# Layer 0 of a two-layer encoder: class heads' logits on the row halves of TensorE, values as the stationary operand on its column halves, head factors spread over channels through DRAM

## The chip, the core and the metric

The kernel runs on one core of one Trainium2 chip. A core has TensorE (PE; its weight loads are listed apart as PEld), VectorE (DVE), ScalarE (ACT), GpSimd (POOL) and SyncE (SP), whose queue issues nearly all of this kernel's transfers. TensorE multiplies a stationary operand that was loaded into its array (128 rows by 128 columns) by a moving operand and writes to PSUM; the other engines read PSUM and work in SBUF. The metric is the device time of one execution in microseconds, the median of several runs.

## The reference, cut to what matters

The input is 512 tokens of 1024 channels. Each of two layers is RMSNorm, a token mixer, a residual add, RMSNorm, a squared-ReLU MLP and a residual add; a final RMSNorm ends the network. The change lies in the mixer of layer 0, dilated sliding-window attention with 16 heads of 64 channels in three groups:

```python
A_GROUPS = ((128, 1, 6), (512, 4, 5), (2048, 16, 5))   # window, dilation, heads
# per group: keys at offsets -win/2 .. win/2 in steps of the dilation, a bias from rel_bias
lse = jax.nn.logsumexp(logits, axis=-1)
p = jnp.exp(logits - lse[..., None])
o = jnp.einsum('bhqk,bqkhd->bqhd', p, v_sel)
glses.append(jax.nn.logsumexp(lse, axis=-1) - math.log(nh))
...
alpha = jax.nn.softmax(jnp.stack(glses, axis=-1), axis=-1)
o = concatenate([outs[g] * (3 * alpha[..., g])[..., None, None] for g in range(3)])
return o.reshape(B, S, 16 * 64) @ w_o
```

So each head's output row (one token) is scaled by one factor, which needs the sums of all 16 heads at that token: the group's weight alpha times three, over the head's own softmax sum.

## The kernel before

**Linear products.** Activations are kept transposed, channels on partitions and the 512 tokens along the free axis, in eight tiles. A weight unit is 1 MB (1024 rows by 256 columns): SP loads it into `raw` (two buffers), ScalarE casts the high part `whi` (L156), VectorE subtracts the low part `wlo` (L157), and TensorE runs three products of 512 columns per step (`mm3`, L167 to L169) into a PSUM bank, `acc` (two banks) or `s_ps` (three).

**Heads in pairs.** The 16 heads are eight pairs p, two heads of 64 channels on one 128-partition tile. Pairs 0 to 2 are the window heads (dilation 1), pairs 3 to 7 the class heads: there tokens are sorted into four classes by their position modulo 4, so that a class of 128 queries meets a class of 128 keys. `qk0(j)` makes queries and keys of pairs 2j and 2j+1, `probs0(p)` the probabilities, `values0(j)` the values and the value products.

**Probabilities.** For a class head, `probs0` runs four products into one `s_ps` bank (L517, the head's 64 partitions as rows of the array, so half of it), one per class b; then per class VectorE adds the bias and takes a minimum, ScalarE takes the exponential and its sum (`softmax_block`); TensorE transposes the four blocks (L523) and VectorE copies them into `pt`, which has keys on partitions and queries along the free axis. Window heads do the same with two blocks of keys per class of queries.

**Values.** `out_v` scales the values, transposes them (L538, four 128x128 blocks), ScalarE copies them to `vn` (L540). The value product has `pt` as the stationary operand, 128x128, and 64 columns of `vn` as the moving one, so the result has queries on partitions (L548 for window heads, two products added up; L552 for class heads). ScalarE copies the bank `o_ps` (one buffer) to `o` (L555).

**Factors and output.** `group_stats` and `head_factors` make the factors with queries on partitions; the statistics of window and class heads sit in different token orders and are exchanged through small DRAM tiles (`exN`, `exS`, L606 to L618). The factors end in `sN` (window heads) and `sS` (class heads), a value per query, block and head. Then, per pair, VectorE multiplies `o` by the factors (L627), TensorE transposes the result back to channels on partitions (L630, four blocks), ScalarE casts the high part `oh` out of PSUM in the reference's token order (L638), VectorE subtracts the low part `ol` (L639), and the output projection `w_o` starts on them.

**Order.** A scheduler with a time model sets the order of instructions on every engine when the kernel is built; on the chip each engine runs its own in that order and waits on semaphores. Tiles come from pools with a fixed number of buffers, and the scheduler keeps the order in which they are asked for.

Of the kernel before, what the change touches and what calls it, by code (L numbers as in the profile page):

```python
# [82 lines left out]
def tile_encoder(ctx: ExitStack, tc: tile.TileContext, x, rel_bias, gains, norm_final_g,  # L83
# [383 lines left out]
    sN = l0p.tile([P, NB, 6], F32, name="sN", bufs=1)  # L467
    mnS = l0p.tile([P, NB, 10], F32, name="mnS", bufs=1)
    sS = l0p.tile([P, NB, 10], F32, name="sS", bufs=1)
# [15 lines left out]
    def probs0(p):  # L485
        for hh in range(2):
            h = 2 * p + hh
            rows = slice(64 * hh, 64 * hh + 64)
            q, k = qT[p], kT[p]
# [21 lines left out]
            else:  # L511
# [3 lines left out]
                S = s_tile().rearrange("p (u k) -> p u k", u=4)  # L515
                for b in range(NB):
                    nc.tensor.matmul(S[:, b, :], q[rows, b * P:(b + 1) * P], k[rows, (3 - b) * P:(4 - b) * P],  # L517
                                     start=True, stop=True)
                for b in range(NB):
                    softmax_block(S[:, b, :], Pt[:, b, :], B1[:, i, :], mnS[:, b, i:i + 1], sS[:, b, i:i + 1])  # L520
# [6 lines left out]
    def values0(j):  # L527
        def out_v(ct, ps):
# [12 lines left out]
            ops = o_tile().rearrange("p (b h e) -> p b h e", b=NB, h=2)  # L541
            for hh in range(2):
                h = 2 * p + hh
                pt = PT[h]
                for b in range(NB):
                    if p < 3:
                        for u in range(2):
                            nc.tensor.matmul(ops[:, b, hh, :], pt[:, 2 * b + u, :],  # L548
                                             v[:, (2 - b + u) % 4, 64 * hh:64 * hh + 64],
                                             start=u == 0, stop=u == 1)  # L550
                    else:
                        nc.tensor.matmul(ops[:, b, hh, :], pt[:, b, :], v[:, 3 - b, 64 * hh:64 * hh + 64],  # L552
                                         start=True, stop=True)
            o = hpool.tile([P, NB, 2, 64], F32, tag=f"Bl{p}", name=f"o{p}")
# [65 lines left out]
    head_factors(allN, [(sN, 0, 6, 0)])  # L620
    values0(2)
# [3 lines left out]
    for p in range(8):  # L625
        f = sN[:, :, 2 * p:2 * p + 2] if p < 3 else sS[:, :, 2 * p - 6:2 * p - 4]
        nc.vector.tensor_mul(O[p], O[p], bcast(f, 64))  # L627
        T = t_tile()
        for b in range(NB):
            nc.tensor.transpose(T[:, b * P:(b + 1) * P], O[p][:, b, :, :].rearrange("p h e -> p (h e)"), ident)  # L630
# [355 lines left out]
```

## Time and profile before

| | us |
|---|---|
| median of 3 runs | 1221.16 (1220.15 to 1221.30) |
| the profiled execution, its own time | 1220.61 |
| span in the trace | 1218.4 |
| TensorE busy | 1203.0 |
| VectorE busy | 628.9 |
| ScalarE busy | 500.6 |

The span runs from the first to the last instruction in the trace; the execution's time has 2.2 us more around it. Busy times count an instruction from start to end, and TensorE's overlap in its pipeline, so a busy time near the span tells that it rarely stands still and not how fast it could be. What a piece of work costs is read from the chain that ended last, in which each piece counts only what it adds.

### The profile page before, as it was taken

To read this page: it belongs to the slowest core of one execution; us is meant where nothing else is said; L and a number is where in the kernel's file an instruction comes from. 1 tells how busy PE (TensorE), PEld (TensorE's weight loads), DVE (VectorE), ACT (ScalarE), POOL (GpSimd) and SP (SyncE) were. 2 spreads that over 40 slices of the span, in tenths; PEclk is the share of its full clock that TensorE was granted. 3 is DMA by queue.
4 is the path that set the end of the run, shared out by engine and by line. 5 is a ranking of instruction groups with operands and counts; after the bars stand their busy time and mean duration, and the time that the engine had idled before them with its cause. 6 is when DMAs were issued, how large, how long until landed. Compare 5 with 4: busy or idle time off the path is not lost.

```text
span 1218.4 us, 15236 instructions
## 1 busy us (share of the span) xinstructions
PE 1203.0 (99%) x6124; PEld 1020.3 (84%) x6124; DVE 628.9 (52%) x1052; ACT 500.6 (41%) x922; POOL 87.5 (7%) x145
## 2 busy tenths in 40 slices
PE   9999999999999999999999999999999999999997
PEld 7788878888888888888888998987888888888897
DVE  5684455744433434434478677675744344334323
ACT  5462333443422413313357676654543224123133
POOL 0000000200000000000101212122200000000012
PEclk9999999999999999999999999999999999999999
DMA  7631222233322333223522333221333322333211
GB/s 226 117 104 36 70 70 70 73 100 104 104 89 84 104 104 104 94 80 104 150 75 94 100 115 107 74 85 54 102 104 104 104 88 86 104 105 104 88 51 70
DMA packets 107478, 115.72 MB, mean 95 GB/s; under 512 B 4703, under 2 KB 101087, under 8 KB 107359
## 3 DMA queue, kind: packets, MB, share of 16 engines
q1 hardware_dynamic: 107344, 114.48, 29.8%
q8 instruction: 48, 0.79, 0.3%
q0 software_dynamic: 64, 0.27, 0.1%
q14 instruction: 22, 0.18, 0.1%
HBM read 112.50 MB, written 2.24 MB: 94 GB/s over the span
## 4 chain that ended last, share of the span: by engine, by line
PE 95%; DMA 2%; DVE 1%; ACT 1%; issue 0%; POOL 0%; POOLq 0%; ACTq 0%; DVEq 0%
PE acc L167 15%; PE acc L169 15%; PE acc L168 15%; PE s_ps L167 13%; PE s_ps L168 13%; PE s_ps L169 13%; PE o_ps L833 2%; DMA raw<-in_a_w_qkv_dram 2%; PE s_ps L349 1%; PE s_ps L350 1%; PE t_ps L824 1%; PE o_ps L548 1%; PE s_ps L517 1%; PE o_ps L552 1%; PE t_ps L508 1%; PE t_ps L130 0%
## 5 line engine op out<-in xcount | busy, mean ns | idle before, releaser
L156 ACT CAST whi<-raw 128x1024 fp32r<-128x1024 f32 x188 | 188.3, 1049 | 399.1 <-PE s_ps L168 201.6
L157 DVE TENSOR_TENSOR wlo<-raw,whi 128x1024 fp32r<-128x1024 f32 x188 | 224.3, 1231 | 28.4 <-ACT whi L156 27.7
L167 PE MATMUL acc<-Ah,whi 128*128 128x512 f32 x472 | 185.5, 393 | 0.0
L168 PE MATMUL acc<-Al,whi 128*128 128x512 f32 x472 | 185.4, 393 | 0.0
L169 PE MATMUL acc<-Ah,wlo 128*128 128x512 f32 x472 | 185.1, 392 | 0.0
L167 PE MATMUL s_ps<-Ah,whi 128*128 128x512 f32 x352 | 137.4, 391 | 0.0
L168 PE MATMUL s_ps<-Al,whi 128*128 128x512 f32 x352 | 137.2, 390 | 0.0
L169 PE MATMUL s_ps<-Ah,wlo 128*128 128x512 f32 x352 | 136.9, 390 | 0.0
L169 PEld LDWEIGHTS acc<-Ah,wlo 128*128 128x128 f32 x472 | 88.7, 188 | 18.3
L167 PEld LDWEIGHTS acc<-Ah,whi 128*128 128x128 f32 x472 | 88.7, 188 | 18.1
L168 PEld LDWEIGHTS acc<-Al,whi 128*128 128x128 f32 x472 | 88.7, 188 | 17.6
L674 ACT ACTIVATE u<-u 128x512 f32<-128x512 f32 x64 | 40.0, 628 | 96.6 <-DVE u L673 95.9
L167 PEld LDWEIGHTS s_ps<-Ah,whi 128*128 128x128 f32 x352 | 66.1, 188 | 14.9 <-ACT Ah L230 0.5
L683 DVE TENSOR_TENSOR h<-h,s_ps 128x512 f32<-128x512 f32 x33 | 22.7, 687 | 108.0 <-PE s_ps L169 108.0
L168 PEld LDWEIGHTS s_ps<-Al,whi 128*128 128x128 f32 x352 | 66.1, 188 | 14.0 <-DVE lsum L392 0.5
L169 PEld LDWEIGHTS s_ps<-Ah,wlo 128*128 128x128 f32 x352 | 66.1, 188 | 13.7
L243 POOL TENSOR_TENSOR nacc<-nacc,nsq 128x512 f32<-128x512 f32 x18 | 27.4, 1525 | 548.5 <-ACT nsq L241 548.0
L673 DVE SCALAR_TENSOR_TENSOR u<-s_ps,rB 128x512 f32<-128x512 f32 x38 | 26.2, 691 | 76.0 <-PE s_ps L169 73.9
L168 PE MATMUL s_ps<-Bl,whi 128*128 128x512 f32 x152 | 59.1, 389 | 0.0
L167 PE MATMUL s_ps<-Bh,whi 128*128 128x512 f32 x152 | 59.1, 389 | 0.0
L169 PE MATMUL s_ps<-Bh,wlo 128*128 128x512 f32 x152 | 59.1, 389 | 0.0
L808 ACT ACTIVATE p<-p,st 128x512 f32<-128x512 f32 x64 | 46.2, 723 | 27.8 <-DVE st L805 27.0
(241 smaller groups left out, 2265.1 us busy)
## 6 DMA issues: line engine op xcount, KB each, us to landing
raw<-in_mlp_w_in_dram SPq DMA_DIRECT2D x32, 1024.0 KB, 5.3
raw<-in_mlp_w_out_dram SPq DMA_DIRECT2D x32, 1024.0 KB, 5.2
raw<-in_b_w_qkv_dram SPq DMA_DIRECT2D x12, 1024.0 KB, 5.1
raw<-in_a_w_qkv_dram SPq DMA_DIRECT2D x10, 1024.0 KB, 5.3
bias<-fd SPq DMA_DIRECT2D x16, 448.0 KB, 3.7
raw<-in_a_w_o_dram SPq DMA_DIRECT2D x4, 1024.0 KB, 5.1
raw<-in_b_w_o_dram SPq DMA_DIRECT2D x4, 1024.0 KB, 5.5
h<-in_x_dram SPq DMA_DIRECT2D x8, 256.0 KB, 4.1
```

Source lines behind the costliest of these rows:

```text
L156: nc.scalar.copy(hi[:, :, c], raw[:, :, c])
L157: nc.vector.tensor_sub(lo[:, :, c], raw[:, :, c], f32(hi[:, :, c]))
L167: nc.tensor.matmul(ps, ahi, bhi, start=first, stop=False)
L168: nc.tensor.matmul(ps, ahi, blo, start=False, stop=False)
L169: nc.tensor.matmul(ps, alo, bhi, start=False, stop=last)
L243: eng.tensor_add(self.acc, self.acc, sq)
L349: nc.tensor.matmul(S, q[m][:, qs], k[m][:, ks], start=True, stop=False)
L673: nc.vector.scalar_tensor_tensor(u, ps, 0.0, nm.rB, op0=ALU.max, op1=ALU.mult)
L674: nc.scalar.activation(u, u, AF.Square)
L683: nc.vector.tensor_add(hT[ct], hT[ct], ps)
L808: nc.scalar.activation(pt, xt, AF.Exp, bias=mn, scale=-1.0, accum_out=st[:, b, 2 + m:3 + m])
L833: marks["PV"] = nc.tensor.matmul(O[:, b, :], aT[:, k, :], v[:, k, es], start=k == 0, stop=k == NB - 1)
```

## The change

Four things change, all in layer 0.

1. For class heads, the logits of both heads of a pair are issued ahead of the two softmaxes, in turn: class b of the head on partitions 0 to 63, then of the head on 64 to 127. They go to two `s_ps` banks.
2. In the value product, the values are now the stationary operand (128 rows by 64 columns) and `pt` the moving one (128 columns). The result has channels on partitions. The two heads of a pair go to partitions 0 to 63 and 64 to 127 of one bank, so to the two column halves of the array, in turn.
3. The transposes of `o` (L630) go, since `o` has channels on partitions already.
4. The factors must therefore run along the free axis, the same for all 64 channels of a head. `sN` and `sS` become parts of one tile `sA`; TensorE transposes it once (64 rows: 16 heads by 4 blocks), ScalarE copies that to `fT`, SP writes it to a DRAM tile `fac`, and eight loads read it back, each row repeated on 64 partitions, into four tiles `fB` of two pairs each. `fB` uses the buffers of the window heads' `ptn`. The product with `o` is written over `fB`, and `oh` and `ol` are made from there, not from PSUM.

```diff
-    sN = l0p.tile([P, NB, 6], F32, name="sN", bufs=1)
+    sA = l0p.tile([P, 16, NB], F32, name="sA", bufs=1)
+    sN = sA[:, 0:6, :].rearrange("p h b -> p b h")
+    sS = sA[:, 6:16, :].rearrange("p h b -> p b h")
-    sS = l0p.tile([P, NB, 10], F32, name="sS", bufs=1)
...
+        if p >= 3:
+            S2 = [s_tile().rearrange("p (u k) -> p u k", u=4) for _ in range(2)]
+            for b in range(NB):
+                for hh, rows in enumerate((lo64, hi64)):
+                    nc.tensor.matmul(S2[hh][:, b, :], q[rows, b * P:(b + 1) * P], k[rows, (3 - b) * P:(4 - b) * P],
+                                     start=True, stop=True)
...
-                S = s_tile().rearrange("p (u k) -> p u k", u=4)
-                for b in range(NB):
-                    nc.tensor.matmul(S[:, b, :], q[rows, b * P:(b + 1) * P], k[rows, (3 - b) * P:(4 - b) * P],
-                                     start=True, stop=True)
...
-            ops = o_tile().rearrange("p (b h e) -> p b h e", b=NB, h=2)
-            for hh in range(2):
-                h = 2 * p + hh
-                pt = PT[h]
-                for b in range(NB):
-                    if p < 3:
-                        for u in range(2):
-                            nc.tensor.matmul(ops[:, b, hh, :], pt[:, 2 * b + u, :],
-                                             v[:, (2 - b + u) % 4, 64 * hh:64 * hh + 64],
-                                             start=u == 0, stop=u == 1)
-                    else:
-                        nc.tensor.matmul(ops[:, b, hh, :], pt[:, b, :], v[:, 3 - b, 64 * hh:64 * hh + 64],
-                                         start=True, stop=True)
+            ops = o_tile()
+            for b in range(NB):
+                for u in range(2 if p < 3 else 1):
+                    for hh, rows in enumerate((lo64, hi64)):
+                        if p < 3:
+                            a, w, last = PT[2 * p + hh][:, 2 * b + u, :], v[:, (2 - b + u) % 4, rows], u == 1
+                        else:
+                            a, w, last = PT[2 * p + hh][:, b, :], v[:, 3 - b, rows], True
+                        nc.tensor.matmul(ops[rows, b * P:(b + 1) * P], w, a, start=u == 0, stop=last)
...
+    fac = dram.tile([64, P], F32, name="fac")
+    T = t_tile()
+    nc.tensor.transpose(T[0:64, 0:P], sA.rearrange("p h b -> p (h b)"), ident)
+    fT = l0p.tile([64, P], F32, name="fT", bufs=1)
+    nc.scalar.copy(fT, T[0:64, 0:P])
+    nc.sync.dma_start(fac, fT)
+    F = []
+    for pp in range(4):
+        f = l0p.tile([P, 2, SEQ], F32, tag="ptn", name="fB", bufs=4)
+        for hh, rows in enumerate((lo64, hi64)):
+            a = fac[0:1, 0:1]
+            nc.sync.dma_start(f[rows], bass.AP(tensor=a.tensor, offset=a.offset + (4 * pp + hh) * SEQ,
+                                               ap=[[0, 64], [2 * SEQ, 2], [1, SEQ]]))
+        F += [f[:, 0, :], f[:, 1, :]]
     values0(2)
     values0(3)
...
-        f = sN[:, :, 2 * p:2 * p + 2] if p < 3 else sS[:, :, 2 * p - 6:2 * p - 4]
-        nc.vector.tensor_mul(O[p], O[p], bcast(f, 64))
-        T = t_tile()
-        for b in range(NB):
-            nc.tensor.transpose(T[:, b * P:(b + 1) * P], O[p][:, b, :, :].rearrange("p h e -> p (h e)"), ident)
+        nc.vector.tensor_mul(F[p], O[p], F[p])
...
-            vh, vl, tv = rev(hi[:, :]), rev(lo[:, :]), T
+            vh, vl, tv = rev(hi[:, :]), rev(lo[:, :]), F[p]
```

The scheduler sets the order anew. Up to the first class head's logits and from the last quarter of the output projection on, TensorE's order is the same; between them it moves at three places that matter here. Names ahead of the arrow are what is written; numbers in them tell buffers apart. A row stands for one product; in the trace an fp32 product of `s_ps` or `o_ps` is two passes.

The first place is TensorE at the logits of pair 5 (L517 before, L493 after), behind those of pair 4 and the value products of pair 2. Before:

```order
L517 MATMUL s_ps_1285<-k0_1124,q0_1062 128x128 x3
L548 MATMUL o_ps_1169<-vn_1167,ptn_872 128x64 x8
L548 MATMUL o_ps_1169<-vn_1167,ptn_907 128x64 x8
L538 MATMUL t_ps_1215<-ident_84,v0_1213 128x128 x4
L523 MATMUL t_ps_1252<-ident_84,psg_1233 128x128 x4
L517 MATMUL s_ps_1285<-k0_1124,q0_1062 128x128
L517 MATMUL s_ps_1310<-k0_1124,q0_1062 128x128 x4
L167 MATMUL acc_1341<-Ah0_126,whi_1127 128x512
```

After, from the transposes of pair 3's values on (s_ps_1282 is the bank of the pair's first head, s_ps_1283 that of the second):

```order
L541 MATMUL t_ps_1214<-ident_84,v0_1212 128x128 x4
L526 MATMUL t_ps_1256<-ident_84,psg_1242 128x128
L493 MATMUL s_ps_1283<-k0_1123,q0_1061 128x128 x2
L526 MATMUL t_ps_1256<-ident_84,psg_1242 128x128
L493 MATMUL s_ps_1283<-k0_1123,q0_1061 128x128
L493 MATMUL s_ps_1282<-k0_1123,q0_1061 128x128
L526 MATMUL t_ps_1256<-ident_84,psg_1242 128x128
L493 MATMUL s_ps_1283<-k0_1123,q0_1061 128x128
L526 MATMUL t_ps_1256<-ident_84,psg_1242 128x128
L167 MATMUL acc_1340<-Ah0_126,whi_1126 128x512
```

The five products that stood in one run now stand in three, with single transposes between. The heads of pairs 4 and 6 alternate as written; those of pairs 3 and 7 stand head by head, as before.

The second place is TensorE behind the linear products of pair 6's values (acc_1709 before, acc_1726 after), where the value products of pair 4 (heads 8 and 9, pt8 and pt9) stand. Before:

```order
L169 MATMUL acc_1709<-Ah7_133,wlo_1605 128x512
L538 MATMUL t_ps_1683<-ident_84,v0_1681 128x128 x4
L552 MATMUL o_ps_1645<-vn_1643,pt8_1234 128x64 x4
L552 MATMUL o_ps_1645<-vn_1643,pt9_1259 128x64 x4
L167 MATMUL acc_1754<-Ah0_126,whi_1604 128x512
```

After:

```order
L169 MATMUL acc_1726<-Ah7_133,wlo_1622 128x512
L624 MATMUL t_ps_1603<-ident_84,sA_514 64x128
L541 MATMUL t_ps_1655<-ident_84,v0_1653 128x128 x4
L553 MATMUL o_ps_1662<-pt8_1243,vn_1660 64x128
L553 MATMUL o_ps_1662<-pt9_1263,vn_1660 64x128
```

The factors' transpose comes in, and behind it the transposes of pair 4's own values (v0_1653), which stood 23 rows earlier before; there the transposes at this place were those of pair 5's values. On VectorE, the low parts of the first unit of output weights (L157, twice) stood ahead of the last step on the window heads' factors, and stand behind it now.

The third place is the start of the output projection on TensorE, and SP's queue for it. Before, behind the last transposes of values:

```order
L538 MATMUL t_ps_1781<-ident_84,v0_1779 128x128 x4
L630 MATMUL t_ps_1800<-ident_84,o0_807 128x128 x4
L552 MATMUL o_ps_1788<-vn_1786,pt14_1508 128x64 x4
L552 MATMUL o_ps_1788<-vn_1786,pt15_1533 128x64 x4
L630 MATMUL t_ps_1810<-ident_84,o1_861 128x128 x4
L167 MATMUL s_ps_1904<-oh0_1805,whi_1702 128x512
L167 MATMUL acc_1933<-oh0_1805,whi_1702 128x512
```

After:

```order
L553 MATMUL o_ps_1707<-pt11_1313,vn_1705 64x128
L541 MATMUL t_ps_1753<-ident_84,v0_1751 128x128 x4
L168 MATMUL acc_1771<-Al7_141,whi_1621 128x512
L169 MATMUL acc_1771<-Ah7_133,wlo_1622 128x512
L167 MATMUL s_ps_1881<-oh0_1817,whi_1719 128x512
L168 MATMUL s_ps_1881<-ol0_1818,whi_1719 128x512
```

And on SP, lines removed and added:

```order
 L617 DMA exS<-allS 512x1x4
 L618 DMA allN<-exS 128x4x4
-L153 DMA raw<-in_a_w_o_dram 128x8x256 x2
+L153 DMA raw<-in_a_w_o_dram 128x8x256
+L627 DMA fac<-fT 64x128
+L633 DMA fB<-fac 64x2x512 x8
+L153 DMA raw<-in_a_w_o_dram 128x8x256
```

The output projection now starts right behind the linear products of pair 7's values, with the value products of pairs 6 and 7 placed among its own; the nine transfers of the factors stand between the third and the fourth load of output weights. On VectorE the products with the factors of pairs 0 to 4 stand ahead of pair 7's values and of the low parts of the second unit of output weights; on ScalarE the casts `oh` of pairs 0 to 2 stand ahead of the copy of pair 5's `o_ps`.

## Rows read from the trace of the kernel before

**Rows 1.** The page of the kernel before, parts 1, 4 and 5: busy time of each engine (share of the span, instructions), the share of each engine in the chain that ended last, and the group of the weights' splits on VectorE (busy us, mean ns of one | idle time before).
```profile
PE 1203.0 (99%) x6124; PEld 1020.3 (84%) x6124; DVE 628.9 (52%) x1052; ACT 500.6 (41%) x922; POOL 87.5 (7%) x145
...
PE 95%; DMA 2%; DVE 1%; ACT 1%; issue 0%; POOL 0%; POOLq 0%; ACTq 0%; DVEq 0%
...
L157 DVE TENSOR_TENSOR wlo<-raw,whi 128x1024 fp32r<-128x1024 f32 x188 | 224.3, 1231 | 28.4 <-ACT whi L156 27.7
```

**Rows 2.** Busy time by stretch over the stretches of layer 0's attention (us from the span's start). Columns: length, busy us (and instructions) of PE, PEld, DVE, ACT, POOL, then the granted TensorE clock as a share of full speed, the share of the DMA engines, and GB/s.
```profile
100.00:140.00 40.00, 40.00 (x245) 34.60 (x244) 20.04 (x56) 12.97 (x35) 0.00 (x0) 1.00 0.24 80
...
170.00:200.00 30.00, 29.70 (x175) 25.23 (x176) 19.87 (x51) 11.61 (x29) 0.00 (x0) 1.00 0.15 44
200.00:230.00 30.00, 29.89 (x148) 24.24 (x147) 13.73 (x16) 12.95 (x16) 1.32 (x1) 1.00 0.11 36
```

**Rows 3.** The chain that ended last, in order of time, around the first value products, from 85 to 132 us: start, us it added to the chain, what (a run of equal pieces in one row).
```profile
85.16 1.08 PE s_ps L517 x8
86.24 0.43 PE acc L169
86.67 0.24 PE acc L167
...
89.00 0.44 PE t_ps L538 x4
...
91.51 3.52 PE o_ps L548 x32
```

**Rows 4.** The same chain, from 128 to 140 us (three heads' logits in one run).
```profile
129.09 1.97 PE s_ps L517 x22
```

**Rows 5.** The same chain, from 160 to 202 us (the rows there, the longest pieces).
```profile
161.90 1.64 PE s_ps L517 x16
...
167.79 0.41 PE s_ps L517 x2
168.21 0.37 PE t_ps L523 x2
```

**Rows 6.** The same chain, from 186 to 206 us.
```profile
192.67 1.73 PE o_ps L552 x16
```

**Rows 7.** The instructions of a line (L548 and L552: the value products; L630: the transposes that go; L517: the class heads' logits; L248: a product with one moving column), each in an answer of its own. Columns: count, ns of one as least/median/most, first and last start, form (rows*columns of the array, moving elements).
```profile
L548 PEld LDWEIGHTS o_ps<-vn,ptn x96: 186/192/193, 91.2 to 134.4; 128*128 128x128 f32 x96
L548 PE MATMUL o_ps<-vn,ptn x96: 217/275/324, 91.3 to 134.5; 128*128 128x64 f32 x96
...
L552 PE MATMUL o_ps<-vn,pt x80: 217/275/323, 139.8 to 200.5; 128*128 128x64 f32 x80
...
L630 PE MATMUL t_ps<-ident,o x32: 270/272/282, 197.8 to 217.4; 128*128 128x128 f32 x32
...
L517 PE MATMUL s_ps<-k,q x80: 272/272/374, 85.1 to 169.7; 64*128 64x128 f32 x80
...
L248 PE MATMUL t_ps<-ones,nacc x32: 164/250/251, 29.6 to 866.7; 128*128 128x1 f32 x32
```

**Rows 8.** Instructions of TensorE in order of time, 197 to 201.5 us: start, us, instruction, and in brackets the idle time before it and what ended it.
```profile
197.84 0.60 PE L630 MATMUL t_ps<-ident,o 128*128 128x128 f32 x4
198.74 2.00 PE L552 MATMUL o_ps<-vn,pt 128*128 128x64 f32 x16 [0.29 <-ACT vn L540]
```

**Rows 9.** The same view of lines of ScalarE and VectorE (count, ns as least/median/most): L540 the copy of the values out of PSUM, L638 the cast to the high part, L627 the product with the factors, L639 the low part.
```profile
L540 ACT COPY vn<-t_ps x8: 567/586/594, 89.5 to 198.1; 128x512 f32<-128x512 f32 x8
...
L638 ACT CAST oh<-t_ps x8: 585/1111/1120, 198.6 to 217.7; 128x512 fp32r<-128x512 f32 x8
...
L627 DVE TENSOR_TENSOR o<-o,sS x5: 681/692/693, 177.4 to 201.4; 128x512 f32<-128x512 f32 x5
...
L639 DVE TENSOR_TENSOR ol<-t_ps,oh x8: 682/1126/1136, 199.5 to 218.8; 128x512 fp32r<-128x512 f32 x8
```

**Rows 10.** DMA issues: tensors, queue, count, KB of each, median us from issue to landing.
```profile
raw<-in_a_w_o_dram SPq DMA_DIRECT2D x4, 1024.0 KB, 5.1
...
h<-in_x_dram SPq DMA_DIRECT2D x8, 256.0 KB, 4.1
...
out_dram<-ot SPq DMA_DIRECT2D x8, 256.0 KB, 2.2
B<-fd SPq DMA_DIRECT2D x1, 768.0 KB, 12.0
B<-fd SPq DMA_DIRECT2D x2, 320.0 KB, 19.0
...
fd<-fsb SPq DMA_DIRECT2D x1, 128.0 KB, 2.6
...
exN<-allN SPq DMA_DIRECT2D x1, 4.0 KB, 4.4
...
exS<-allS SPq DMA_DIRECT2D x1, 8.0 KB, 3.4
```

More of the change, by code (lines that the diff above doesn't have):

```diff
@@ L485, in probs0 @@
     def probs0(p):
+        q, k = qT[p], kT[p]
+        if p >= 3:
[4 more added lines that the diff above has]
+                                     start=True, stop=True)
         for hh in range(2):
             h = 2 * p + hh
-            rows = slice(64 * hh, 64 * hh + 64)
-            q, k = qT[p], kT[p]
             if p < 3:
@@ L514, in probs0 @@
                 pt = hpool.tile([P, NB, P], F32, tag=f"Bh{h % 8}", name=f"pt{h}")
-                S = s_tile().rearrange("p (u k) -> p u k", u=4)
                 for b in range(NB):
-                    nc.tensor.matmul(S[:, b, :], q[rows, b * P:(b + 1) * P], k[rows, (3 - b) * P:(4 - b) * P],
-                                     start=True, stop=True)
-                for b in range(NB):
-                    softmax_block(S[:, b, :], Pt[:, b, :], B1[:, i, :], mnS[:, b, i:i + 1], sS[:, b, i:i + 1])
+                    softmax_block(S2[hh][:, b, :], Pt[:, b, :], B1[:, i, :], mnS[:, b, i:i + 1], sS[:, b, i:i + 1])
                 T = t_tile()
@@ L540, in out_v @@
             nc.scalar.copy(v.rearrange("p a b -> p (a b)"), T)
-            ops = o_tile().rearrange("p (b h e) -> p b h e", b=NB, h=2)
-            for hh in range(2):
-                h = 2 * p + hh
-                pt = PT[h]
-                for b in range(NB):
-                    if p < 3:
-                        for u in range(2):
-                            nc.tensor.matmul(ops[:, b, hh, :], pt[:, 2 * b + u, :],
-                                             v[:, (2 - b + u) % 4, 64 * hh:64 * hh + 64],
-                                             start=u == 0, stop=u == 1)
-                    else:
-                        nc.tensor.matmul(ops[:, b, hh, :], pt[:, b, :], v[:, 3 - b, 64 * hh:64 * hh + 64],
-                                         start=True, stop=True)
-            o = hpool.tile([P, NB, 2, 64], F32, tag=f"Bl{p}", name=f"o{p}")
+            ops = o_tile()
[7 more added lines that the diff above has]
+                        nc.tensor.matmul(ops[rows, b * P:(b + 1) * P], w, a, start=u == 0, stop=last)
+            o = hpool.tile([P, SEQ], F32, tag=f"Bl{p}", name=f"o{p}")
             nc.scalar.copy(o, ops)
@@ L633, in tile_encoder @@
         if p < 3:
-            vh, vl, tv = rev(hi[:, :]), rev(lo[:, :]), T
+            vh, vl, tv = rev(hi[:, :]), rev(lo[:, :]), F[p]
         else:
             vh, vl, tv = (rev(hi.rearrange("p (m c) -> p c m", c=4)), rev(lo.rearrange("p (m c) -> p c m", c=4)),
-                          T.rearrange("p (c m) -> p c m", c=4))
+                          F[p].rearrange("p (c m) -> p c m", c=4))
         nc.scalar.copy(vh, tv)
```

## The prediction

> **What bounds the kernel now.** I read the page first: TensorE is busy for 1203.0 of 1218.4 us and makes 95% of the chain that ended last [rows 1]. Then the stretches of layer 0's attention: TensorE is busy 29.7 us or more of every 30, and the granted clock is 1.00, the 2.4 GHz level, throughout [rows 2]. So here a microsecond of TensorE's own work is a microsecond of the kernel, as long as no wait takes its place. The chain in order of time then gives the price of each piece, because it counts what an instruction adds and not how long it lasts in the pipeline.
>
> In those rows four transposes add 0.44 us, so 0.11 each; a 512-column product adds 0.24; 32 passes of the value products (16 products, each fp32 product being two passes) add 3.52, 0.11 each [rows 3]. A value pass has only 64 moving columns. Its weight load of 128 columns lasts 186 to 193 ns, and a pass with a single moving column lasts nearly as long in the median (250 ns against 275) [rows 7], so the load sets the 0.11 and not the columns. The shortest passes say what columns cost: 164 ns with one column, 217 with 64 [rows 7], 0.84 ns a column by my estimate, so 0.107 us for 128 columns. The value passes are bound by loading, and turning them round (64 loaded, 128 moving) makes them bound by moving, at the same 0.11, unless two halves run at once.
>
> **Value products, all eight pairs.** Before, there are 96 + 80 = 176 passes [rows 7], at 0.11 each 19.5 us, all on the chain (16 passes add 1.73 in a quiet place [rows 6]). After, as many passes, but heads alternate on the two column halves in every pair. No column half is used in the trace before, so the price is bounded. Upper end: nothing overlaps, 0.11 a pass, 0 saved. Lower end: both halves at once, 88 x 0.11 = 9.7 us, 9.8 saved. The nearest row is the class heads' logits on row halves. 16 passes of two heads add 1.64 where one head's 8 add 1.08 [rows 3, 5], and 22 passes of three heads add 1.97 [rows 4]; at 0.11 and nothing overlapped it would be 1.95 and 2.6. So this array does run two halves at once in fp32, even where the order gives four products of one head and then four of the other. I take the lower end, -9.8.
>
> The price of changing the array's shape shows there too. Eight logits passes add 1.08 and not 0.88, and the product behind them 0.43 and not 0.24: 0.39 for a visit [rows 3]; between transposes and logits it is 0.41 + 0.37 for four passes worth 0.44, so 0.34 [rows 5]. Eight visits, one of which already follows logits: 7.5 x 0.39 = **+2.9** (ends 2.4 and 2.9). The second half starts behind the first, by up to one pass: 8 x 0.06 = **+0.5** (ends 0 and 0.9).
>
> The Trainium skill, "TensorE: Matmul & The Clock Gate", Part 3, measured 2.38 times the speed with three column tiles, 79% of full. By that the passes would take 19.5 / 1.59 = 12.3 us, an estimate, and the sum below would be 2.6 smaller; no run here shows it.
>
> **Transposes.** 32 of them go [rows 7], 0.11 each: -3.5. The one of the factors comes: +0.1. Net **-3.4**.
>
> **Logits.** The order shows that the turn of row halves survives in two of five pairs. Pair 6: 16 passes become 8 steps of 0.11 and 0.2 for the way in, 1.1 against 1.64: -0.55. Pair 4 with three products of pair 5 behind it: the busier half has 14 passes, 1.75 against 1.97: -0.2. Pairs 3 and 7 stand as before: 0. Pair 5 is split by single transposes into three visits instead of one: two more visits are 0.78, less some overlap, +0.7. Net **0** (-0.5 to +0.4).
>
> **Waits on TensorE.** Before pair 7 it idles 0.29 for the copy of the values [rows 8]; in the new order other work lies there, -0.3. But the factors' transposes now stand ahead of those of pair 4's values, and pair 4's products right behind these, with nothing between: TensorE waits for a hand-over, a copy of 0.59 and a hand-over [rows 9], **+0.8**. Net +0.5. The transposes of factors also wait for VectorE's last factor step; TensorE gets there only after pair 6's linear products, and in VectorE's queue the two weight splits that stood ahead of that step now stand behind it. I cost this at 0; if they ran first all the same, it would be up to their 2 x 1.23 = 2.5 [rows 1].
>
> **The way through DRAM.** From the factors' transposes to the first output product stand 12 transposes (1.3), that wait (0.8), two value groups (2 x 1.27) and 24 products of 0.24 (5.7): 10.3 us. In it must pass: a copy of at most 0.59; the write, 2.6 to 4.4 by the three small writes to DRAM, 3.4 by the one nearest in size and place; the load of the first pair of tiles, 2.2 to 4.1 by the 256 KB transfers, say 3.2; the product 0.69 and the cast 0.59 [rows 9, 10], and some 0.5 of hand-overs. That is 9.0, with ends near 7 and 11.5. The second tile lands up to 2.6 us later (half a megabyte at the rate of 1 MB in 5.1 [rows 10]), and its first use comes 12 products (2.9 us) after. So I take 0 and keep +3 as the far end, since behind the waiting products on VectorE stand pair 7's values and the split of the next output weights, and behind the waiting cast on ScalarE pair 5's copy out of PSUM and that split's other part, for which TensorE would wait in turn. On SP's queue the nine transfers stand ahead of one 1 MB load of output weights only, and this one is needed over 100 products later: 0. The products with the factors (0.69) and the casts and low parts (0.59 to 1.14) [rows 9] are as many and as large as before, beside TensorE: 0.
>
> **Sum.** -9.8 + 2.9 + 0.5 - 3.4 + 0 + 0.5 + 0 = **-9.3 us**. The profiled execution took 1220.61 and would take 1211.3; the median, 1221.16, lies 0.55 above it: 1211.9, so 1212. With the ends of the small terms: 1209.5 to 1216.
>
> **Rivals.**
> - *Half an overlap.* The halves overlap only as far as the logits' 4-and-4 order does (1.64 for 16 passes, about 0.09 each without the way in): 176 x 0.02 = 3.5 saved instead of 9.3. Sum -3.5: 1217.5. Against it: here the halves alternate at every product.
> - *No overlap.* Both halves need all 128 rows for their own moving data, which the row halves do not; if they take turns, the sum is 0 + 2.9 - 3.4 + 0.5 = 0: 1221. Nothing in the trace excludes it.
> - *The factors come late (slower).* The place is the first output product. Loads out of a small DRAM tile took 12.0 and 19.0 us in this trace [rows 10]. If the first tile takes 19.0 and not 3.2, TensorE stands for 15.8 less the 1.3 of cover, 14.5: 1226. It decides from a landing of 4.5 us on, and from about 14 us on the kernel is slower than before. Against it: those loads ran beside the first weights, with DMA at seven tenths; here its share is 0.15 [rows 2].
> - *Loads that don't hide (slower).* In the full array the next load hides behind a running product: spacing is 0.11 where load and product last 0.19 and 0.28 [rows 7]. If it did not on column halves, a pass would take 0.107 and half a load, about 0.055: 176 x 0.16 = 28.2 against 19.5, the sum +8.7: 1230. The rule for this stands in the Trainium skill, "TensorE: Matmul & The Clock Gate", Part 3, by which loads overlap running products only where the row group differs; the trace speaks against it, since in the full array it does not differ.
>
> **How the numbers follow.** Full overlap 0.64 (1209.5 to 1216), half 0.12 (1216 to 1219.5), none 0.14 (1220 to 1223), late factors 0.07 (1217 to 1228), loads that don't hide 0.03 (1226 to 1231). About 0.2% (2.4 us) is what a measurement can tell from no change, so faster is below 1218.7: 0.64 + 0.09 + 0.01 = 0.74; slower is above 1223.6: 0.09; same 0.17. The range 1209.5 to 1221.5 leaves out part of the third case and most of the last two.
>
> **What would show it.** In the chain after, a window pair's 32 value passes should add about 2 us and a class pair's 16 about 1.1, with the product behind at 0.43; no transposes of o are left; TensorE idles about 0.8 for pair 4's copy; and the first output product waits for ScalarE's cast under 1 us. I am wrong if the value passes stay at 0.11 each, or if a wait for the factors of several microseconds stands ahead of the output products.

## The result

| | before | changed | ratio |
|---|---|---|---|
| median | 1221.23 us (1220.15 to 1222.04, 4 runs) | 1213.5 us (1211.44 to 1215.84, 4 runs) | 0.9939 [0.9927, 0.9951] |
| profiled execution | 1220.61 us (span 1218.4) | 1211.44 us (span 1209.7) | |
| again (below) | 1221.81 us (15 runs) | 1212.80 us (1211.82 to 1213.69, 5 runs) | 0.9929 [0.9917, 0.9942] |

Forecast were 1212 us, with 1209.5 to 1221.5 as the range. The profile agrees on most terms of the sum and disagrees on one. The page of the changed kernel, busy time and chain (it answers to [rows 1]): TensorE has 11.5 us less to do, and DMA and SyncE's queue appear in its chain.

```profile
PE 1191.5 (99%) x6093; PEld 1005.9 (83%) x6093; DVE 629.3 (52%) x1052; ACT 500.8 (41%) x923; POOL 87.4 (7%) x145
...
PE 94%; DMA 3%; DVE 1%; ACT 1%; issue 0%; SPq 0%; POOL 0%; POOLq 0%; ACTq 0%; DVEq 0%
```

The chain of the changed kernel in order of time, 85 to 132 us (it answers to [rows 3, 4]):

```profile
91.01 1.90 PE o_ps L553 x32
...
125.65 1.75 PE s_ps L493 x22
...
129.31 0.59 PE t_ps L541 x4
130.00 0.64 PE s_ps L493 x4
130.64 0.26 PE t_ps L526
130.90 0.42 PE s_ps L493 x4
...
131.58 0.41 PE s_ps L493 x2
```

A window pair's 32 value passes add 1.90 us where they added 3.52, and the 22 logit passes of pair 4 and of three products of pair 5 1.75 where they added 1.97. The last rows are the price of pair 5's split: 10 logit passes in three pieces, 0.64 + 0.42 + 0.41, and transposes at 0.26 each instead of 0.11 between them. The same chain from 132 to 210 us (it answers to [rows 5, 6]):

```profile
136.60 1.02 PE o_ps L553 x16
...
156.65 1.09 PE s_ps L493 x16
...
179.92 4.59 DMA fac<-fT
184.57 0.62 SPq L633
...
187.84 6.32 DMA fB<-fac
```

A class pair's 16 value passes add 1.02 (1.73 before), pair 6's 16 logit passes 1.09 (1.64 before). Then the chain leaves TensorE: the write of the factors (4.59 us), the loads' issues on SyncE's queue one behind the other, 0.6 us each, and a load of 6.32, the sixth of the eight. SyncE's queue there:

```profile
179.10 0.37 SPq L153 DMA_DIRECT2D raw<-in_a_w_o_dram  x1
179.92 0.51 SPq L627 DMA_DIRECT2D fac<-fT  x1
184.57 5.57 SPq L633 DMA_DIRECT2D fB<-fac  x8
200.41 0.39 SPq L153 DMA_DIRECT2D raw<-in_a_w_o_dram  x1
```

The third weight load is issued 0.8 us ahead of the write and lands at 184.24, the write right behind it at 184.51. The eight loads land from 188.37 to 196.19, and no weight load is under way beside them. What all this does to TensorE is in its instructions with idle time ahead of them, 178 to 198 us:

```profile
180.71 1.09 PE L553 MATMUL o_ps<-pt,vn 128*64 128x128 f32 x16 [0.68 <-ACT vn L543]
...
191.04 0.50 PE L167 MATMUL s_ps<-oh,whi 128*128 128x512 f32 x1 [1.57 <-ACT oh L649]
...
191.76 0.50 PE L168 MATMUL s_ps<-ol,whi 128*128 128x512 f32 x1 [0.22 <-DVE ol L650]
```

The idle 0.68 is pair 4's copy, as forecast. The 1.57 was forecast at under 1 us and costed at nothing. The same place in busy time by stretch (it answers to [rows 2], where 170 to 200 us held 29.70 us of TensorE and a DMA share of 0.15):

```profile
170.00:200.00 30.00, 27.25 (x160) 20.83 (x159) 17.71 (x33) 11.52 (x18) 0.00 (x0) 1.00 0.44 107
```

### The profile page after: what moved, and what is told of

It reads as the page before. It is cut to its first block, busy times and chain, and to the rows that moved or that the text cites. A ratio compares the mean times of both kernels' runs of the same rounds, so it can differ in the third digit from the quotient of the medians.

```text
span 1209.7 us, 15193 instructions
## 1 busy us (share of the span) xinstructions
PE 1191.5 (99%) x6093; PEld 1005.9 (83%) x6093; DVE 629.3 (52%) x1052; ACT 500.8 (41%) x923; POOL 87.4 (7%) x145
## 4 chain that ended last, share of the span: by engine, by line
PE 94%; DMA 3%; DVE 1%; ACT 1%; issue 0%; SPq 0%; POOL 0%; POOLq 0%; ACTq 0%; DVEq 0%
PE acc L169 15%; PE acc L168 15%; PE acc L167 15%; PE s_ps L168 13%; PE s_ps L167 13%; PE s_ps L169 13%; PE o_ps L844 2%; DMA raw<-in_a_w_qkv_dram 2%; PE s_ps L349 1%; PE s_ps L350 1%; PE t_ps L835 1%; PE s_ps L493 1%; PE o_ps L553 1%; DMA fB<-fac 1%; PE t_ps L515 1%; PE t_ps L130 0%
## 5 line engine op out<-in xcount | busy, mean ns | idle before, releaser
L157 DVE TENSOR_TENSOR wlo<-raw,whi 128x1024 fp32r<-128x1024 f32 x188 | 224.6, 1232 | 28.4 <-ACT whi L156 27.7
L816 DVE CUSTOM_DVE_ANT_0 p<-s_ps,bias 128x512 f32<-128x512 f32 x64 | 43.3, 688 | 27.9 <-PE s_ps L350 20.8
```

Source lines behind the costliest of these rows:

```text
L157: nc.vector.tensor_sub(lo[:, :, c], raw[:, :, c], f32(hi[:, :, c]))
L816: nc.vector.tensor_tensor_reduce(out=xt, in0=S, in1=bias[h][m][:, b * P:b * P + SEQ], scale=1.0, scalar=3.0e38, op0=ALU.add, op1=ALU.min, ...
```

## The experiments

Two theories stood at the start. **A:** the gain is two passes at once on column halves and 32 transposes less; the loss is the factors' way through DRAM. **B:** the overlap belongs to the halves and not to the turns, or the logits' turns carry a part, and the wait for the factors is only cover for work that comes anyway.

Executions of one kernel scatter by up to 4.5 us, and one wait at the span's start, which the change doesn't touch (TensorE for VectorE's mnN), was 2.3 to 5.5 us long in these profiles. So beside each median stands a **stretch** of the profiled execution that leaves start and end out: from the first transposes of pair 0's values to the last output product of layer 0, both read as start times in TensorE's timeline (before: 88.84 to 247.90; changed: 88.33 to 238.76).

| kernel | median us | ratio to before | stretch us |
|---|---|---|---|
| before | 1221.2 to 1222.4 | | 159.1 |
| changed | 1213.50 | 0.9939 [0.9927, 0.9951] | 150.4 |
| changed, again | 1212.80 | 0.9929 [0.9917, 0.9942] | 151.2 |
| values by head | 1219.43 | 0.9983 [0.9974, 0.9993] | 156.4 |
| turns by two | 1214.22 (one) | | 153.5 |
| logits by head | 1212.42 | 0.9924 [0.9912, 0.9937] | 151.0 |
| logits alone | 1221.22 | 0.9995 [0.9986, 1.0004] | 158.6 |
| transposes back | 1217.00 | 0.9962 [0.9949, 0.9974] | 155.0 |
| factors filled | 1209.23 | 0.9900 [0.9886, 0.9913] | 147.3 |
| visits doubled | 1226.83 | 1.0044 [1.0030, 1.0058] | 164.4 |
| loads split | 1213.02 | 0.9929 [0.9915, 0.9942] | 152.0 |
| factors early | 1216.16 | 0.9963 [0.9950, 0.9977] | 154.2 |
| early and cover | 1212.15 | 0.9925 [0.9912, 0.9937] | 151.7 |
| cover alone | 1215.18 | 0.9947 [0.9935, 0.9959] | 152.3 |

**Values by head.**

```diff
-            for b in range(NB):
-                for u in range(2 if p < 3 else 1):
-                    for hh, rows in enumerate((lo64, hi64)):
+            for hh, rows in enumerate((lo64, hi64)):
+                for b in range(NB):
+                    for u in range(2 if p < 3 else 1):
```

> The changed kernel with its value products in the order of heads: same column halves, same stationary values, same 176 passes, but all of one head and then all of the other. Theory of the prediction (taking turns is what lets two passes share 0.11 us): only the one pass at the border between the two heads of a pair can overlap, so about 88 x 0.109 - 8 x 0.109 = 8.7 us come back: 1220 against 1211.4 to 1213.5 of the changed kernel; a window pair's 32 products take about 3.4 us instead of 1.9, a class pair's 16 about 1.8 instead of 1.0. Rival (the halves alone do it, whatever the order, or the gain is that of the removed transposes): within 1 us of the changed kernel, 1.9 and 1.0 us as there.

The chain, a window pair and a class pair:

```profile
131.69 3.26 PE o_ps L553 x32
...
143.09 1.51 PE o_ps L553 x16
```

The gain goes with the turns: 1219.43 is 5.9 to 6.6 us above the changed kernel's two medians, and the stretch is 5.2 to 6.0 longer. By the rows it is 3 x 1.36 + 5 x 0.49 = 6.5, while TensorE's wait for the factors (on oh) is 0.9 shorter here (0.7 for 1.57). It is less than the 8.7 expected, because a border, the place where one head's passes end and the other's begin, hides more than one pass. At 0.11 a pass (3.52 for 32) and with 0.14 for the way in and out (1.90 less 16 x 0.11), nothing overlapped would be 3.66 and 1.90; 3.26 and 1.51 are 0.40 and 0.39 less, 3.6 passes for one border.

**Turns by two** puts that to the test with three borders a pair: turns of 8 passes in a window pair, of 4 in a class pair.

```diff
+            for half in range(2):
+                for hh, rows in enumerate((lo64, hi64)):
+                    for b, u in [(b, u) for b in (2 * half, 2 * half + 1) for u in range(2 if p < 3 else 1)]:
```

> The changed kernel with its value products in turns of 4 (a window pair: 8 products of one head, then 8 of the other, twice: 16 passes a turn are cut to 8) and of 2 (a class pair: 2 products, which are 4 passes). Head by head, about 3.4 passes overlapped at the border of two heads: the trace showed the second head's first passes start beside the first head's last ones. Theory now (TensorE starts a pass on the free half some 3 to 4 passes ahead of the one that is running, so that each border hides that much): a class pair has three borders and 16 passes in turns of 4, nearly all hidden: 1.0 to 1.15 us, as one by one; a window pair has three borders in turns of 8: 32 passes in about 2.45 us (3.6 less 3 x 3.4 x 0.109), between 1.9 and 3.26. Rival (only passes that take turns one by one overlap): a class pair 1.5 us and more, a window pair 3.2.

```profile
128.24 2.50 PE o_ps L553 x32
...
138.48 1.07 PE o_ps L553 x16
```

3.66 less 2.50 is 1.16, three borders of 0.39. Turns of four passes (the class pair) overlap nearly whole, 1.07 against 1.02; the rival's 1.5 and 3.2 are far off. So half an overlap and no overlap, the two likeliest rivals of the prediction, are both out for the changed kernel's order, and what decides is the length of a turn.

**Logits by head**, the logits' part undone in the changed kernel, and **logits alone**, that part put into the kernel before.

```diff
-            for b in range(NB):
-                for hh, rows in enumerate((lo64, hi64)):
-                    nc.tensor.matmul(S2[hh][:, b, :], ...
+                S2[hh] = s_tile().rearrange("p (u k) -> p u k", u=4)
+                rows = (lo64, hi64)[hh]
+                for b in range(NB):
+                    nc.tensor.matmul(S2[hh][:, b, :], ...
```

> The changed kernel with the class heads' logits made as before, four of one head and then four of the other. Theory of the prediction (the logits' turns are worth about nothing, since what pairs 4 and 6 gain pair 5 loses): within 0.8 us of the changed kernel, either way. Rival (logits gain as the values do): 40 logit products lose a half of 0.11 us each, 2.2 us slower, 1214 to 1216.

> The kernel before with one part of the change alone: the class heads' logits of a pair in turn on the two row halves, into two PSUM tiles. Theory of the prediction (sum 0, between -0.5 and +0.4 us): 1220.5 to 1221.6, the 16 logit passes of pair 6 in 1.1 us instead of 1.6, given back where the scheduler cuts another pair's row of logits in pieces. Rival (turns gain a half of 0.11 us for each of 40 products): 1219 or less.

The chain of logits by head, pairs 4 (with three products of 5), 5 (its last 10 passes) and 6:

```profile
126.74 1.97 PE s_ps L521 x22
...
131.52 0.41 PE s_ps L521 x2
132.19 1.09 PE s_ps L521 x8
...
157.88 1.64 PE s_ps L521 x16
```

Turned, the first and last are 1.75 and 1.09, 0.77 less. What pair 5 gives back is seen in its four transposes, ten logit passes and the linear product behind them: 1.96 in the kernel before, where the ten passes stand in one run, 2.59 in the changed kernel, and 2.52 here, where they are split too. So by the rows the turns are worth 0.14 beside the kernel before and 0.7 beside this one; in logits alone pair 5 stays in one run, and 0.77 should be won. 1212.42 against 1212.80, and 1221.22 against 1221.81: neither can be told from nothing. In the stretches logits by head lies between the changed kernel's two profiles (151.0; 150.4 and 151.2), with a shorter wait for the factors (1.0 for 1.57), and logits alone is 0.5 shorter than the kernel before. The rival's 2.2 us is out.

**Transposes back.**

```diff
         nc.vector.tensor_mul(F[p], O[p], F[p])
+        T = t_tile()
+        for b in range(NB):
+            nc.tensor.transpose(T[:, b * P:(b + 1) * P], F[p][:, b * P:(b + 1) * P], ident)
```

> The changed kernel with the 32 transposes of the outputs put back: four of each product of output and factor, into the tiles in which they used to go, read by nothing. Theory of the prediction (they lay on TensorE's path, 32 x 0.106 = 3.4 us): 3 to 3.8 us slower than the changed kernel, 1216 to 1217. Rival (TensorE has idle time there that takes them in): under 1 us slower.

1217.00, 4.2 above the changed kernel's second median, a little more than the 3 to 3.8 expected, and 3.9 in the stretch beside its second profile (155.02 less 151.16). Of that, 0.4 is a longer wait for the factors ahead of the first of these transposes (2.0 for 1.6); 3.5 are left, 0.11 for each transpose, as forecast. They lie on the path.

**Factors filled** takes the DRAM loads away, and the factors with them: the tiles hold ones.

```diff
-            a = fac[0:1, 0:1]
-            nc.sync.dma_start(f[rows], bass.AP(...))
+            nc.gpsimd.memset(f[rows], 1.0)
```

> The changed kernel in which the tiles of factors are filled with one on GpSimd and not loaded from DRAM; the eight loads are left out, and the factors with them, while the transpose, its copy, the write to DRAM and VectorE's eight products stay. Theory (the way through DRAM costs what TensorE waits ahead of the first output products, 1.57 + 0.22 + 0.20 us and a little): 1.8 to 2.3 us faster than the changed kernel, no wait of TensorE on ScalarE's cast above 0.3 us. Rival (the wait is cover for work that comes later anyway, so that it turns up in another place): within 0.5 us of the changed kernel.

TensorE's waits, the whole list (columns: who <- whom, us in total, times, longest):

```profile
PE s_ps L349 <- DVE mnN L475: 5.5, 1, 5.5
PE t_ps L130 <- POOL ident masks.py:199: 2.5, 1, 2.5
PE o_ps L842 <- ACT aT L835: 2.1, 2, 1.4
PE o_ps L553 <- ACT vn L543: 0.7, 1, 0.7
```

The waits on oh and ol are gone and nothing takes their place. The stretch is 3.1 us shorter than the changed kernel's, 3.9 shorter than in that kernel's second profile, and the median is lower by 3.6 (of 1212.80). That is more than the 2.0 of listed idle time from which 1.8 to 2.3 was expected. One part of the rest is seen in TensorE's timeline of the changed kernel, where the value products of pair 6 end the first row of output products:

```profile
197.19 1.09 PE L553 MATMUL o_ps<-pt,vn 128*64 128x128 f32 x16
```

20 output products stand between 191.04 and 197.19, and 20 x 0.23 is 4.6 of these 6.15 us: 1.5 lost, where the list has 0.42. Each product that starts from a standstill takes 0.50 and not 0.40, and short pauses are not listed. 1.57 + 1.5 is the 3.1 of the stretch.

**Changed, again** was run as a measure and showed the clock.

> The changed kernel once more, as the measure for the kernels run beside it. Both theories: 1211 to 1215, as at first.

Stretches of 2 us around the wait for the factors (the granted clock is the number behind the five engines), two of the first profile and three of the second:

```profile
190.00:192.00 2.00, 0.74 (x2) 0.43 (x3) 1.71 (x4) 1.22 (x2) 0.00 (x0) 1.00 1.07 230
192.00:194.00 2.00, 1.80 (x8) 1.13 (x8) 1.81 (x3) 1.32 (x3) 0.00 (x0) 1.00 1.07 238
...
190.00:192.00 2.00, 0.88 (x6) 0.45 (x4) 0.88 (x2) 0.15 (x1) 0.00 (x0) 1.00 1.05 233
192.00:194.00 2.00, 1.26 (x3) 0.81 (x4) 1.66 (x3) 1.07 (x2) 0.00 (x0) 0.89 1.06 229
194.00:196.00 2.00, 2.00 (x6) 1.61 (x5) 1.61 (x4) 1.78 (x3) 0.00 (x0) 0.50 1.06 228
```

In the second profile TensorE had been busy for 0.88 and 1.26 of 2 us; then the granted clock fell to 0.50, the 1.2 GHz level, for some 3 us, and came back (0.75 from 196 to 198, then 1.00). In the first profile, with 0.74 and 1.80, it stayed at 1.00. Instructions and order are the same, and the stretch is 0.7 us longer (151.2 against 150.4). The clock also fell to 0.50 or 0.51 at this place in the profiles of loads split, turns by two, visits doubled, transposes back, early and cover, and cover alone, and in factors early behind that kernel's own long wait; it did not in factors filled, nor where the wait on oh was 0.7 us (values by head) or 1.0 (logits by head). So a part of the executions of the changed kernel pays for the wait twice. In how many, these runs don't say.

**Visits doubled.**

```diff
             for b in range(NB):
+                if b == 2:
+                    nc.tensor.matmul(ops[:, P:3 * P], ident, t[:, 0:256], start=True, stop=True)
                 for u in range(2 if p < 3 else 1):
```

> The changed kernel with one product over the full array (128x256, single precision) put between the two halves of each pair's value products, eight in all; it overwrites the outputs of one block of 128 tokens, so that block's values are left out of the result. Each costs its own run time of about 0.21 us, 1.7 us together. Theory of the prediction (each going from full array to column halves and back costs 0.39 us beside the work): 8 x (0.21 + 0.39) = 4.8 us slower than the changed kernel. Rival (the change of shape costs nothing; the 0.2 us steps in the trace are the tail of the last product): 1.7 us slower.

The chain, first pair, and further on where the factors land:

```profile
90.44 1.02 PE o_ps L555 x16
91.47 0.63 PE o_ps L548 x2
92.09 1.02 PE o_ps L555 x16
...
191.66 6.39 DMA fB<-fac
198.15 0.69 DVE fB L643
198.84 0.98 DVE v L538
199.87 1.11 PE t_ps L541 x4
```

One more visit makes 1.90 into 1.02 + 0.63 + 1.02, 0.77 more. The product in it is two passes of 256 columns (I had counted one): by 0.11 for 128 columns an estimate of 0.44, so the visit itself is 0.33 and not 0. Eight times 0.77 is 6.2; the kernel became 13.3 us longer in the stretch than in the changed kernel's second profile. The other 7 came unasked: the scheduler put VectorE's factor product ahead of pair 6's values, that product waited for a load of 6.39 us, the values behind it, and TensorE behind these, and the clock fell: TensorE was busy 0.94, 0.83 and 0.67 of 2 us from 194 to 200, and the granted clock was 0.50 from 200 to 204. It is the prediction's fear of what is queued behind the waiting product, in full size. The trace gives the price of a visit; the kernel's time says nothing of it.

**Loads split.** Four kernels tried to mend the wait. The first shortens the first load.

```diff
+        for i0, n in ([(0, 1), (1, 1)] if pp == 0 else [(0, 2)]):
             for hh, rows in enumerate((lo64, hi64)):
-                nc.sync.dma_start(f[rows], ...
+                (nc.sync, nc.gpsimd)[hh].dma_start(f[rows, i0:i0 + n, :], ...
```

> The changed kernel with the loads of the spread factors cut otherwise: pair 0's and pair 1's in transfers of their own (64 x 512, 128 KB), and the lower half of the channels issued from SyncE's queue, the upper half from GpSimd's. Theory (TensorE's 2 us wait is the first tile's way: the second issue on SyncE, 0.62 us behind the first, and 256 KB in each): both halves of pair 0 are issued at once as the write has landed and land 3.3 to 3.8 us later, the wait falls to 0.7 us or less, the kernel is 0.8 to 1.5 us faster than the changed one. Rival (the landing is set by what else the DMA engines carry, a weight tile of 1024 KB among it, or GpSimd's queue is slower to start): the wait stays within 0.4 us of 1.6, or grows.

TensorE's waits:

```profile
PE s_ps L168 <- DVE ol L652: 1.7, 2, 1.5
...
PE s_ps L167 <- ACT oh L651: 0.4, 1, 0.4
```

The first wait fell as theory A had it, from 1.6 to 0.4: the small loads landed in 3.1 and 3.3 us (medians of two on each queue). But a wait of 1.5 stands on a later tile now: the loads of 256 KB took 7.1 and 7.3 us in the median instead of 5.5, and the last of all landed 11.0 us after the first was issued, against 11.6. Nothing was won: 1213.02. On the wait A was right for the first tile and wrong for the kernel, because it forgot the later ones.

**Factors early** and **early and cover** start the way sooner and the output products later, by edges that order two instructions of one engine: the output products behind pair 6's value products, pair 7's transposes too, and VectorE's products with the factors in an order of their own. **Cover alone** does the same but for the sooner start.

```diff
+    turn = nc.tensor.transpose(T[0:64, 0:P], sA.rearrange("p h b -> p (h b)"), ident)
+    values0(2, hooks=[(5, lambda: behind.append(turn))])     # early and cover: 13
...
+            if first and later:
+                st.enter_context(tc.issue_after(later[0].ins))
             nc.tensor.matmul(ps, ahi, bhi, start=first, stop=False)
...
+        ahead = [v_mul[6]] if p == 0 else [fs[p - 1]] + ols[:p - 1][-1:] + ([v_mul[7]] if p == 2 else [])
...
+    later.append(v_mm[6])
```

> The changed kernel with the way of the factors begun earlier and covered longer, by edges of order alone: TensorE's transpose of the factors goes ahead of the sixth of eight steps of pair 4's value projection (2 us sooner), the first output product goes behind pair 6's value products, pair 7's value transposes behind these, and VectorE's eight products keep their own order with pair 7's tile ahead of the third. Theory (the loss is the factors' landing, 2 us of idle TensorE and, in some executions, a clock that falls to its lower level behind it for 3 us, which costs 1.5 us more): no wait of TensorE on ScalarE's cast or VectorE's difference above 0.4 us, granted clock 1.00 through 190 to 200 us, and 2 to 3.6 us faster than the changed kernel: 1209 to 1211. Rival (the loads land later when they start earlier beside the weight tile, or the wait turns up at pair 7's transposes): within 1 us of the changed kernel, 1212 to 1214.

> The kernel of the run before with the transpose of the factors in a later place: there it stood so early that TensorE waited 4.6 us for the factors themselves; here it stands three steps ahead of the end of pair 5's value projection, 2.05 us ahead of where the changed kernel has it. The later start of the output products (behind pair 6's value products) and VectorE's order stay. Theory (the loss is the factors' landing and the clock that can fall behind it): TensorE waits under 0.4 us on the outputs' casts, clock 1.00 there, 2 to 3.6 us faster than the changed kernel, 1209 to 1211. Rival (every order has its own waits, and the changed kernel's is near the best): within 1 us of it, 1212 to 1214, with the wait at the factors' transpose or at pair 7's value transposes.

> The same with the transpose of the factors where the changed kernel has it; only the cover is longer: pair 6's value products (1.0 us with their step) stand ahead of the first output product. Theory: 1.0 to 1.2 us of the 2 us wait are filled, 0.8 to 1.0 us stay, 1 us or, with the clock's fall gone, up to 2.5 us faster than the changed kernel: 1210 to 1212. Rival: within 0.5 us of the changed kernel, since pair 7's tile now waits behind VectorE's products with the factors.

TensorE's timeline of each, in this order, the row with the long wait:

```profile
176.67 0.27 PE L634 MATMUL t_ps<-ident,sA 128*64 128x128 f32 x1 [4.58 <-DVE sA L600]
```

```profile
193.83 1.97 PE L563 MATMUL o_ps<-pt,vn 128*64 128x128 f32 x16 [2.25 <-ACT o L565]
```

```profile
194.18 1.09 PE L563 MATMUL o_ps<-pt,vn 128*64 128x128 f32 x16 [3.37 <-ACT vn L553]
```

In all three the waits on oh and ol are gone, and another stands in their place. Factors early put the transpose ahead of its own data. The other two wait on ScalarE, whose copies of pairs 5 to 7 stand behind its casts of the factor products. ScalarE's timeline in early and cover:

```profile
190.29 0.62 ACT L663 CAST oh<-fB 128x512 fp32r<-128x512 f32 x1
190.82 0.59 ACT L553 COPY vn<-t_ps 128x512 f32<-128x512 f32 x1
191.30 1.99 ACT L156 CAST whi<-raw 128x1024 fp32r<-128x1024 f32 x2
193.19 0.59 ACT L565 COPY o<-o_ps 128x512 f32<-128x512 f32 x1
```

The copy for which TensorE idles 2.25 us comes behind a cast, another pair's copy and the next weights' two casts. Here the rival was right: early and cover, at 0.9925, is level with the changed kernel (0.9929). The other two came out slower than theory and rival alike had it: factors early at 0.9963, and cover alone at 0.9947, where the intervals still touch. No version beat it by more than these runs can tell; what is left to win, by factors filled, is 3 to 4 us.

One thing changed in two of them beside what was meant to. SyncE's queue in early and cover:

```profile
179.38 0.50 SPq L637 DMA_DIRECT2D fac<-fT  x1
181.25 6.47 SPq L643 DMA_DIRECT2D fB<-fac  x8
```

The third weight load stands behind the factors here, as in factors early, and in both the write landed after 1.8 us. In every other kernel with this write the weight load is issued ahead of it, and the write lands 0.2 to 1.0 us behind that load, after 3.5 to 5.6 us. A kernel that moves only this load was not run. By these rows it would take 2.8 us off the factors' way of 11.7 and leave 8.9, less than the 10.1 of cover: an estimate, which leaves out that the weight tile then lands later (9.5 and 10.3 us after its issue in these two).

## Why the prediction was nearly right

Two lines of the chain before, which belong beside [rows 3, 6, 8]:

```profile
131.06 3.71 PE o_ps L548 x32
...
195.67 1.91 PE o_ps L552 x16
```

- **Value products, -9.8:** right in the mechanism, both halves at once, and -9.0 in size. Three times 1.90 and five times 1.02 are 10.80; before, the eight rows were 3.52, 3.52, 3.71, three times 1.73, 1.91 and 2.00, together 19.85 (the forecast's 19.5 were 176 times 0.11). The way into eight groups is in the 10.80. The Trainium skill, "TensorE: Matmul & The Clock Gate", Part 3, gives 2.38 times with three column tiles and lets loads overlap only where row groups differ; here two halves gave 1.85 times (3.52 / 1.90) with the way in and out and 2.0 without it, and the loads hid (two of 0.132 to 0.137 us in every 0.11).
- **Visits and the late half, +2.9 and +0.5:** too dear. The rows have 0.14 in each of eight groups (1.1, already in the 10.80) and, where transposes follow, 0.15 behind (0.59 against 0.44, up to 1.2): 2.3 at most, against 3.4. The logits' 0.39, on row halves, was not the price of column halves; 0.33 is what visits doubled gives.
- **Transposes, -3.4:** right. Put back they cost 3.5 without the longer wait; 4.2 by the medians.
- **Logits, 0:** right, and by the forecast pieces: -0.22, -0.55, and pair 5 giving back 0.63 (0.7 forecast), -0.1 together.
- **Waits on TensorE, +0.5:** 0.68 for pair 4's copy where 0.8 was forecast, and pair 7's 0.29 is gone, +0.4. The factors' transpose waited for nobody.
- **The way through DRAM, 0:** this step failed. The sum had 9.0 us under a cover of 10.3. The cover was right: TensorE stood ready at 191.04 - 1.57 = 189.47, 10.1 us after the factors' transpose. The way was 11.7. The write took 4.6 for 3.4: it landed right behind a weight load of 1 MB that was issued ahead of it, and where none was it took 1.8. I had asked what the nine transfers hold up and not what holds them up. The first tile took 5.1 (184.57 to 189.64) for 3.2, because it needs two loads, issued 0.66 apart, which with the six behind them keep the DMA engines full (share 1.04 to 1.07) and land some 1.2 us apart. I had priced a load alone and taken the middle of a range where its upper end, 11.5, was near. The wait then cost 3.1 and not 1.6, as the output products behind it came with pauses between them, tile by tile, and 0.7 more between the two profiles, of which the clock fell in one. The far end, +3, held it.

So the forecast of -9.3 met -9.2 in the profiled execution and -7.7 to -9.0 in the medians because two errors cancel, and that is luck: the value products, visits and transposes gave 1.4 to 2.6 us more than forecast and the DRAM way took 3 to 4. By the terms measured: -9.0, up to +1.2 behind the visits, -3.4, -0.1, +0.4, +3.1 is -9.0 to -7.8; the stretch says -8.6 (159.1 to 150.4), and -7.9 in the profile in which the clock fell. Of the rivals, late factors happened at a fifth of its size; the other three are refuted for this order.

## What to carry to other kernels

Two small products of which each fills one half of TensorE's columns run at once if they take turns in the queue, in short turns: 1.85 times here, and a whole head at a time gave back 5 to 7 of 9 us. A small detour through DRAM is not priced by one transfer alone but by what is issued ahead of its write, the issues, all that is loaded with it, and the in-order queues of VectorE and ScalarE, where copies that TensorE needs sooner stand behind the product that waits. A wait moved is not a wait removed: of five kernels aimed at this one, only the one without the loads won.

## What the runs showed that I had not expected

- A border between two heads hides 0.39 us, 3.6 passes, and not one. The start times in the trace of values by head show how. In pair 2 the passes start 0.11 apart up to 132.98; then eight start within 0.39 us (132.98, 132.99, 133.09, 133.15, 133.20, 133.26, 133.31, 133.37), which are two rows of passes 0.11 apart, one beside the other. So the second head's first pass started while three of the first head's were still to start. Turns of four passes are nearly as good as single ones (1.07 against 1.02).
- Behind a wait of 1.6 us in a TensorE that is otherwise nearly always busy the granted clock fell to 0.50 for some 3 us, and in another execution of the same kernel, at the same place and behind the same wait, it did not (0.50 against 1.00).
- SyncE takes 0.57 to 0.62 us to issue one of these loads (64 partitions, each reading the same two rows of 2 KB), 5.6 us for all eight. They land 0.8 to 1.3 us apart, so 2 MB come in at some 230 GB/s with the DMA engines full (share 1.07).
- A write of 32 KB that was issued 0.5 to 1.9 us behind a load of 1 MB on the same queue landed right behind that load, after 3.5 to 5.6 us, and after 1.8 us where no such load stood ahead of it.
